# Gate and up products of 20 of 22 feature blocks per feed-forward as seven half-size block products instead of eight

## The chip, the cores and the metric

The kernel runs on one core of one Trainium2 chip. The metric is the device time of one execution in microseconds (us). The kernel before takes 1288.24 us, the median of 3 runs that lie between 1288.08 and 1288.88.

A core has engines that run side by side, each with its own queue, which it works through strictly in order: PE multiplies matrices (PEld is its weight load, which overlaps its products), DVE (VectorE), ACT (ScalarE) and POOL (GpSimd) work on elements, SP issues most DMAs. An instruction whose input is not ready holds up everything behind it on its engine.

## The reference, cut to what matters

The reference is an encoder of two layers in float32, for 512 tokens of 1024 features. Each layer is attention and then a feed-forward with 2816 hidden features:

```
def rmsnorm(x, g):
    y = xf * lax.rsqrt(jnp.mean(xf * xf, axis=-1, keepdims=True) + NORM_EPS)
    return y * g

def swiglu(hn, w_in, w_out):
    gate, up = jnp.split(hn @ w_in, 2, axis=-1)
    return (jax.nn.silu(gate) * up) @ w_out

for layer in range(DEPTH):            # 2
    x = x + attention of rmsnorm(x)   # latent + dilated windows in layer 0, grouped queries in layer 1
    x = x + swiglu(rmsnorm(x, ffn_norm[layer]), ffn_w_in[layer], ffn_w_out[layer])
return rmsnorm(x, final_norm)
```

`hn @ w_in` is 512 x 1024 times 1024 x 5632, twice: this is the product that the change computes in another way.

## The kernel before, in words

Features lie on the 128 partitions, the 512 tokens in the free dimension, so a token array is 8 tiles of 128x512. Every product is made from operands in two parts, high and low (`split`, `load`, `mm3` in lines 144 to 167): high x high, high x low, low x high, each a matmul that accumulates into one PSUM bank. Weights come in blocks of 128x1024 by one DMA into `wraw` (2 buffers); ACT makes the high part `whi` (line 154), POOL the low part `wlo` (line 155); `whi` and `wlo` have 3 buffers each.

The feed-forward (`ffn`) goes over 22 blocks of 128 hidden features in three groups of 8, 7 and 7 (`FGROUPS`). For a block f it makes the gate and the up product (`proj`, 24 matmuls of 512 columns each: 8 blocks of input features x 3), multiplies both by `rb` (one over the root mean square of every token, spread over all partitions), applies Silu, and splits the result. After a group come 8 output products with `ffn_w_out`. The gain of the norm is in the inputs already, the root mean square is not: so products start from `x` times gain while the sum of squares is still being added up on POOL, and `rb` comes later. The steps to `rb` are: the squares added (line 196, POOL), summed over partitions (line 213, PE), scaled (line 216, DVE), raised to -1/2 (line 218, POOL), spread (line 225, PE), copied (line 228, ACT).

The last group of layer 1 goes to `tokens_out`, which makes the last output product with tokens on partitions and the final norm.

The order of instructions on each engine is written by a scheduler when the kernel is built, from the program's order, priorities and its own estimates of durations; tiles of one tag share a place, and a new tile of a tag waits until the old one has been read for the last time.

Of the kernel before, what the change touches and what calls it, by code (L numbers as in the profile page):

```python
# [93 lines left out]
def encoder_kernel(ctx: ExitStack, tc: tile.TileContext, a, out):  # L94
# [554 lines left out]
    def ffn(xt, nr, layer, hsets, tail=None):  # L649
        w1, w2 = a["ffn_w_in"][layer], a["ffn_w_out"][layer]  # L650
        xs = nr.parts
        rb = None
        for gi, (f0, f1) in enumerate(FGROUPS):
            hs = []
            for f in range(f0, f1):
                tags = (("s", "s"), ("pt", "acc"))[f] if f < 2 else ("acc", "acc")
                og = proj(load([wview(w1, 0, KB, f * P, (f + 1) * P)], KB), xs, tags[0])
                ou = proj(load([wview(w1, 0, KB, FF + f * P, FF + (f + 1) * P)], KB), xs, tags[1])
                if rb is None:
                    rb = nr.spread(nr.columns(DM))  # L660
# [274 lines left out]
```

## Time and profile before

| | |
|---|---|
| median of 3 runs | 1288.24 us |
| profiled execution, first to last instruction (span) | 1286.2 us |
| what lies around the span, median less span | 2.0 us |
| PE busy | 1265.6 us, 98% of the span |
| DVE busy | 593.6 us, 46% |
| ACT busy | 524.2 us, 41% |
| POOL busy | 656.6 us, 51% |

The times come from three runs without the profiler, the profile from one execution of its own; it has no time beside its span. A row of a timeline gives the start, the duration, the engine, the line, the operation with the tile that it writes and the tiles that it reads, and in brackets how long the engine had been idle and who released it. The matmul rows overlap, since the engine is pipelined: the pace of PE is the distance between two starts, not the duration of one.

### The profile page before, as it was taken

The numbers are of one execution on the slowest core, as the hardware profiler recorded it, in microseconds if no ns is written. First come the engines' busy times: TensorE is split into PE (matmuls) and PEld (weight loads), VectorE is DVE, ScalarE is ACT, GpSimd is POOL, SyncE is SP. The second block draws the span as 40 slices with busy tenths as digits, with TensorE's granted clock in tenths as the row PEclk, the third lists the DMA queues.
The fourth block names the chain that finished last, engine by engine and source line by source line (L and its number), as shares of the span: only waits on it lengthen the run. The fifth ranks groups of instructions, "written<-read, shape, count | busy, mean of one in ns | idle before, by whom it ended". The sixth has DMA issues, their size and how long they took to land.

```text
span 1286.2 us, 15919 instructions
## 1 busy us (share of the span) xinstructions
PE 1265.6 (98%) x5925; PEld 1023.1 (80%) x5925; DVE 593.6 (46%) x1037; ACT 524.2 (41%) x892; POOL 656.6 (51%) x406
## 2 busy tenths in 40 slices
PE   8999999999999999999999999999999999999997
PEld 7877788787788888888889877787788888888886
DVE  4543347975333133213354878997333123313333
ACT  5324346864332123222243577675432123222242
POOL 5644334545644444444466787766644444444450
PEclk9999999999999999999999999999999999999999
DMA  9333333113332333232332520203233233233331
GB/s 281 83 100 108 77 70 109 48 50 92 99 98 82 106 90 96 86 109 87 91 101 86 139 63 23 71 24 94 83 99 97 85 97 99 88 92 98 98 99 66
DMA packets 200717, 117.88 MB, mean 92 GB/s; under 512 B 15890, under 2 KB 192064, under 8 KB 200640
## 3 DMA queue, kind: packets, MB, share of 16 engines
q1 hardware_dynamic: 198864, 113.69, 30.8%
q10 hardware_dynamic: 1776, 3.17, 0.7%
q8 instruction: 47, 0.77, 0.3%
q14 instruction: 30, 0.25, 0.1%
HBM read 106.09 MB, written 4.19 MB: 86 GB/s over the span
## 4 chain that ended last, share of the span: by engine, by line
PE 91%; DVE 3%; POOL 2%; DMA 2%; ACT 1%; issue 1%; SPq 0%; POOLq 0%; ACTq 0%; DVEq 0%
PE ps_acc L165 24%; PE ps_acc L166 24%; PE ps_acc L167 24%; PE ps_pt L338 3%; PE ps_o L366 2%; PE ps_s L166 2%; PE ps_s L167 2%; PE ps_s L165 2%; PE ps_o L365 2%; POOL wlo L155 1%; PE ps_s L825 1%; PE ps_s L826 1%; PE ps_s L490 1%; PE ps_o L522 1%; DMA m<-e 1%
## 5 line engine op out<-in xcount | busy, mean ns | idle before, releaser
L155 POOL TENSOR_TENSOR wlo<-wraw,whi 128x1024 fp32r<-128x1024 f32 (+3 forms) x194 | 444.7, 2295 | 441.3 <-ACT whi L154 438.0
L154 ACT CAST whi<-wraw 128x1024 fp32r<-128x1024 f32 (+3 forms) x194 | 188.4, 971 | 529.3 <-PE ps_acc L166 461.9
L165 PE MATMUL ps_acc<-x,whi 128*128 128x512 f32 x672 | 266.6, 397 | 2.0 <-DVE x L357 1.6
L167 PE MATMUL ps_acc<-x,wlo 128*128 128x512 f32 x672 | 266.5, 397 | 0.0
L166 PE MATMUL ps_acc<-x,whi 128*128 128x512 f32 x672 | 266.4, 397 | 0.0
L165 PE MATMUL ps_acc<-b,whi 128*128 128x512 f32 x448 | 177.1, 395 | 0.0
L166 PE MATMUL ps_acc<-b,whi 128*128 128x512 f32 x448 | 176.6, 395 | 0.0
L167 PE MATMUL ps_acc<-b,wlo 128*128 128x512 f32 x448 | 176.6, 395 | 0.0
L165 PEld LDWEIGHTS ps_acc<-x,whi 128*128 128x128 f32 x672 | 126.4, 188 | 32.3 <-issue 1.4
L166 PEld LDWEIGHTS ps_acc<-x,whi 128*128 128x128 f32 x672 | 126.5, 188 | 29.0 <-DVE x L359 0.4
L167 PEld LDWEIGHTS ps_acc<-x,wlo 128*128 128x128 f32 x672 | 126.5, 188 | 29.0
L664 DVE TENSOR_TENSOR m<-ps_acc,rbc 128x512 f32<-128x512 f32 x42 | 29.0, 691 | 195.9 <-PE ps_acc L167 195.9
L165 PEld LDWEIGHTS ps_acc<-b,whi 128*128 128x128 f32 x448 | 84.0, 187 | 20.6
L167 PEld LDWEIGHTS ps_acc<-b,wlo 128*128 128x128 f32 x448 | 84.0, 187 | 20.6
L166 PEld LDWEIGHTS ps_acc<-b,whi 128*128 128x128 f32 x448 | 84.0, 187 | 20.4
L674 DVE TENSOR_TENSOR d<-d,ps_acc 128x512 f32<-128x512 f32 x40 | 27.5, 688 | 143.0 <-PE ps_acc L167 143.0
L179 DVE TENSOR_TENSOR b<-ps_pt,b 128x512 fp32r<-128x512 f32 x112 | 75.1, 682 | 17.2 <-ACT b L178 16.7
L178 ACT CAST b<-ps_pt 128x512 fp32r<-128x512 f32 x112 | 63.2, 584 | 25.1 <-PE ps_pt L338 24.3
L165 PE MATMUL ps_acc<-d,whi 128*128 128x512 f32 x160 | 63.2, 397 | 0.1
L167 PE MATMUL ps_acc<-d,wlo 128*128 128x512 f32 x160 | 62.5, 393 | 0.0
L196 POOL TENSOR_TENSOR nacc<-nacc,e 128x512 f32<-128x512 f32 x31 | 47.0, 1518 | 26.5 <-ACT e L195 26.0
L662 DVE TENSOR_TENSOR m<-ps_acc,rbc 128x512 f32<-128x512 f32 x40 | 27.7, 691 | 65.2 <-PE ps_acc L167 65.2
(326 smaller groups left out, 2041.2 us busy)
## 6 DMA issues: line engine op xcount, KB each, us to landing
wraw<-in_ffn_w_in_dram SPq DMA_DIRECT2D x88, 512.0 KB, 3.8
wraw<-in_ffn_w_out_dram SPq DMA_DIRECT2D x23, 512.0 KB, 3.5
wraw<-in_w_in_ab_dram SPq DMA_DIRECT2D x21, 512.0 KB, 3.9
wraw<-in_ffn_w_out_dram SPq DMA_DIRECT2D x24, 448.0 KB, 3.4
wraw<-in_gqa_w_q_dram SPq DMA_DIRECT2D x8, 512.0 KB, 3.6
wraw<-in_gqa_w_o_dram SPq DMA_DIRECT2D x16, 192.0 KB, 2.4
bias<-in_c_bias_dram SPq DMA_DIRECT2D x4, 576.0 KB, 4.2
b<-in_x_dram SPq DMA_DIRECT2D x4, 512.0 KB, 6.5
```

The lines of the kernel that those rows point to most:

```text
L154: nc.scalar.copy(h, r)
L155: nc.gpsimd.tensor_sub(l, r, h.bitcast(F32))
L165: nc.tensor.matmul(dst, lhsT=lhs[0], rhs=rhs[0], start=first, stop=False)
L166: nc.tensor.matmul(dst, lhsT=lhs[0], rhs=rhs[1], start=False, stop=False)
L167: nc.tensor.matmul(dst, lhsT=lhs[1], rhs=rhs[0], start=False, stop=last)
L178: nc.scalar.copy(hi, src)
L179: nc.vector.tensor_sub(lo, src, hi.bitcast(F32))
L196: nc.gpsimd.tensor_add(self.acc, self.acc, sq)
L338: nc.tensor.transpose(pt[:, k * P:(k + 1) * P], p[:, k * P:(k + 1) * P], ident)
L662: nc.vector.tensor_mul(gg, og, rb)
L664: nc.vector.tensor_mul(uu, ou, rb)
L674: nc.vector.tensor_add(xt[n], xt[n], o)
```

## The change

Per feed-forward, blocks f = 0 and 1 are computed as before (but with the sign turned); the other 20 by `seven`. It takes gate and up weights of a block as a 2 x 2 matrix (gate or up, input features 0 to 511 or 512 to 1023) and the inputs as another (input features, tokens 0 to 255 or 256 to 511), and uses Strassen's scheme in Winograd's form: seven products of half size, each 4 x 3 matmuls of 256 columns, in place of eight. Sums of weights (`sab`, `sdc`) and of inputs (`combine`) are needed for it. The sums are made in float32 and split afterwards. `combine` needs `rb` before it can start, since the inputs have to be normalised now; it runs once per feed-forward, after block 0. The groups become (0 to 8, 8 to 16, 16 to 22) in layer 0 and (0 to 8, 8 to 14, 14 to 18, 18 to 22) in layer 1, and up to four output products of the last group stand behind a block of the next one.

```
+    def combine(xt, rb, gk):
...
+        cb = {n: [] for n in ("b11", "b21", "b22", "t1", "t2", "t3", "t4")}
+        H = T // 2
+        for i in range(4):
+            g1, g2 = gain(gk, i), gain(gk, i + 4)
+            ya, yb = U(f"m{4 + 2 * (i % 2)}"), U(f"m{5 + 2 * (i % 2)}")
+            nc.vector.tensor_mul(ya, xt[i], rb)
+            nc.vector.tensor_mul(yb, xt[i + 4], rb)
+            y11 = E()[:, 0:H]
+            tt = U(("tab", "bias")[i % 2], shape=((P, 2, T), (P, 9 * P))[i % 2])
...
+            nc.scalar.activation(y11, ya[:, 0:H], AF.Copy, scale=g1)
+            nc.vector.scalar_tensor_tensor(tt[:, 0:H], ya[:, H:T], g1, y11, op0=ALU.mult, op1=ALU.subtract)
+            nc.vector.scalar_tensor_tensor(tt[:, H:T], yb[:, H:T], g2, tt[:, 0:H], op0=ALU.mult, op1=ALU.subtract)
+            nc.vector.tensor_sub(tt[:, T:T + H], y11, tt[:, H:T])
+            nc.vector.scalar_tensor_tensor(tt[:, T + H:2 * T], yb[:, 0:H], g2, tt[:, H:T],
+                                           op0=ALU.mult, op1=ALU.subtract)
...
+            split(bh, bl, y11)
+            cb["b11"].append((bh, bl))
+            h, l = U(f"d{2 * i}", F32R), U(f"d{2 * i + 1}", F32R)
+            nc.scalar.activation(h, yb, AF.Copy, scale=g2)
+            nc.vector.scalar_tensor_tensor(l, yb, g2, h.bitcast(F32), op0=ALU.mult, op1=ALU.subtract)
+            cb["b21"].append((h[:, 0:H], l[:, 0:H]))
+            cb["b22"].append((h[:, H:T], l[:, H:T]))
+            for j in range(2):
+                h, l = U(f"x{4 * i + 2 * j}", F32R), U(f"x{4 * i + 2 * j + 1}", F32R)
+                src = tt[:, j * T:(j + 1) * T]
+                nc.scalar.activation(h, src, AF.Copy, scale=-1.0)
+                nc.vector.scalar_tensor_tensor(l, src, -1.0, h.bitcast(F32), op0=ALU.mult, op1=ALU.subtract)
...
+    def seven(w1, f, cb):
...
+        def parts(src, hi, lo):
+            nc.scalar.copy(hi, src)
+            nc.vector.tensor_sub(lo, src, hi.bitcast(F32))
+            return hi, lo
...
+        rg = U("wraw", bufs=2, shape=(P, WCOLS))
+        nc.sync.dma_start(rg.rearrange("p (k n) -> p k n", k=KB), wview(w1, 0, KB, f * P, (f + 1) * P))
+        u1, u2 = U(f"m{4 + 2 * (f % 2)}"), U(f"m{5 + 2 * (f % 2)}")
+        for h, u in enumerate((u1, u2)):
+            nc.sync.dma_start(u.rearrange("p (k n) -> p k n", k=4),
+                              wview(w1, 4 * h, 4 * h + 4, FF + f * P, FF + (f + 1) * P))
...
+        gh, gl = parts(rg, U("whi", F32R, bufs=3, shape=(P, WCOLS)), U("wlo", F32R, bufs=3, shape=(P, WCOLS)))
+        nc.vector.tensor_add(sab[:, 0], u1, u2)
+        nc.vector.tensor_add(sab[:, 1], sab[:, 0], g1)
+        ah, al = parts(sab.rearrange("p a b -> p (a b)"), U("whi", F32R, bufs=3, shape=(P, WCOLS)),
+                       U("wlo", F32R, bufs=3, shape=(P, WCOLS)))
+        nc.vector.tensor_add(sdc[:, 0], sab[:, 1], g2)
+        nc.vector.tensor_add(sdc[:, 1], u1, g1)
+        dh, dl = parts(sdc.rearrange("p a b -> p (a b)"), U("whi", F32R, bufs=3, shape=(P, WCOLS)),
+                       U("wlo", F32R, bufs=3, shape=(P, WCOLS)))
+        uh, ul = U("oT", F32R, bufs=2), U(("m12", "otmp")[f % 2], F32R)
+        nc.scalar.copy(uh, u2)
+        nc.gpsimd.tensor_sub(ul, u2, uh.bitcast(F32))
...
+        def product(o, h, l, half, name, first):
+            for i in range(4):
+                c = slice(half * T + i * P, half * T + (i + 1) * P)
+                x = cb[name][i]
+                for j, (wt, xp) in enumerate(((h, x[0]), (h, x[1]), (l, x[0]))):
+                    nc.tensor.matmul(o[:, 0:H], lhsT=wt[:, c], rhs=xp, start=first and i == 0 and j == 0,
+                                     stop=i == 3 and j == 2, skip_group_check=True)
...
+        product(r1, gh, gl, 0, "b11", True)
+        nc.scalar.copy(e[:, 0:H], r1[:, 0:H])
+        yield None
+        r2 = psum("acc")
+        product(r2, gh, gl, 1, "b21", True)
+        nc.vector.tensor_add(gg[:, 0:H], r2[:, 0:H], e[:, 0:H])
+        r3 = psum("pt")
+        product(r3, ah, al, 0, "t1", True)
+        nc.scalar.copy(e[:, T:T + H], r3[:, 0:H])
+        product(r1, ah, al, 1, "t2", False)
+        nc.scalar.copy(e[:, H:T], r1[:, 0:H])
+        product(r3, dh, dl, 0, "b22", False)
+        nc.vector.tensor_add(gg[:, H:T], r3[:, 0:H], e[:, H:T])
+        nc.scalar.activation(gg, gg, AF.Silu)
+        product(r1, dh, dl, 1, "t3", False)
+        nc.vector.tensor_add(uu[:, H:T], r1[:, 0:H], e[:, T:T + H])
+        yield None
+        product(r1, uh, ul, 0, "t4", False)
+        nc.vector.tensor_mul(uu[:, 0:H], r1[:, 0:H], gg[:, 0:H])
+        nc.vector.tensor_mul(uu[:, H:T], uu[:, H:T], gg[:, H:T])
+        yield uu
...
+        def finish(f, unit):
+            uu = next(unit)
+            hs[f] = slot(f)
+            split(*hs[f], uu)
...
+        todo, open_ = [], None
+        for gi, (f0, f1) in enumerate(groups):
+            for f in range(max(f0, FIRST), f1):
+                unit = seven(w1, f, cb)
+                next(unit)
+                if open_ is not None:
+                    finish(*open_)
+                next(unit)
+                open_ = f, unit
+                if f > f0:
+                    for _ in range(min(len(todo), 4)):
+                        out_block(*todo.pop(0))
...
     def tokens_out(hs, f0):
...
-                    nc.gpsimd.tensor_sub(t[2 + h], r, t[h].bitcast(F32))
...
+            nc.vector.tensor_sub(t[:, 2:4], r, t[:, 0:2].bitcast(F32))
```

`product` makes 12 matmuls of 256 columns (line 725 of the changed kernel). The inputs of the classic blocks now lie in the large tiles `b0` to `b3` in both layers. Block 2 stands for the first block by `seven` below.

Where it stands on the engines, first PE in layer 0, between the four classic products and what follows them; the rows give line, operation, written tile, read tiles, size, and the engines waited for. Before:

```order
L167 MATMUL ps_acc_3179<-x7_2758,wlo_3175 128x512
L225 MATMUL ps_o_3125<-ident_72,rcol_3123 128x128 [waits Pool_49]
L225 MATMUL ps_o_3125<-ident_72,rcol_3123 128x128 x3
L165 MATMUL ps_acc_3218<-x0_2744,whi_3213 128x512 [waits Activation_49]
L166 MATMUL ps_acc_3218<-x8_2745,whi_3213 128x512
L167 MATMUL ps_acc_3218<-x0_2744,wlo_3214 128x512
```

and now:

```order
L167 MATMUL ps_acc_3271<-b1_2937,wlo_3267 128x512
L225 MATMUL ps_o_3113<-ident_72,rcol_3111 128x128 [waits Pool_49]
L225 MATMUL ps_o_3113<-ident_72,rcol_3111 128x128 x3
L725 MATMUL ps_s_3334<-d16_3141,whi_3314 128x256 [waits DVE_49,Activation_49]
L725 MATMUL ps_acc_3351<-d0_3145,whi_3314 128x256 [waits Activation_49]
L725 MATMUL ps_s_3334<-d17_3142,whi_3314 128x256 [waits DVE_49]
```

Before, PE went straight on to block 2 after line 225, with inputs `x` that it had; now what follows line 225 reads `d16`, `d17`, `d0` and so on, which `combine` writes.

DVE at the same place. Before, `rb` (`rbc`) is used by the multiplications of blocks 0 and 1, and then DVE waits for PE:

```order
L202 SCALAR_TENSOR_TENSOR x15_2759<-d15_2735,gcol_65,x7_2758 128x512 [waits Activation_49]
L216 TENSOR_SCALAR tiny_3121<-ps_o_3116 128x4 [waits PE_49]
L662 TENSOR_TENSOR m8_3132<-ps_s_3060,rbc_3130 128x512 [waits Activation_49]
L664 TENSOR_TENSOR m10_3133<-ps_s_3091,rbc_3130 128x512
L662 TENSOR_TENSOR m9_3204<-ps_pt_3148,rbc_3130 128x512 [waits PE_49]
```

Now a low part of 128x1024 stands ahead of line 216, which is on the way to `rb`:

```order
L695 TENSOR_TENSOR wlo_3315<-wraw_3306,whi_3314 128x1024 [waits PE_49,DMAHW6_49,Activation_49,Pool_49]
L216 TENSOR_SCALAR tiny_3109<-ps_o_3104 128x4 [waits PE_49]
L763 TENSOR_TENSOR m8_3120<-ps_s_3048,rbc_3118 128x512 [waits Activation_49]
L765 TENSOR_TENSOR m10_3121<-ps_s_3079,rbc_3118 128x512
L659 TENSOR_TENSOR m4_3130<-d8_2728,rbc_3118 128x512 [waits DMAHW3_49]
L660 TENSOR_TENSOR m5_3131<-d12_2732,rbc_3118 128x512 [waits DMAHW7_49,DMAHW5_49,DMAHW3_49]
```

and from `m8_3120<-ps_s_3048,rbc_3118`, the first that needs `rb`, to the low part `wlo_3321` DVE has 54 instructions, which end so:

```order
L684 SCALAR_TENSOR_TENSOR x9_3202<-tab_3187,x8_3201 128x512 [waits DMAHW4_49,Activation_49]
L684 SCALAR_TENSOR_TENSOR x13_3227<-bias_3214,x12_3226 128x512 [waits DMAHW0_49,Activation_49]
L684 SCALAR_TENSOR_TENSOR x11_3206<-tab_3187,x10_3205 128x512 [waits Activation_49]
L684 SCALAR_TENSOR_TENSOR x15_3231<-bias_3214,x14_3230 128x512 [waits Activation_49]
L708 TENSOR_TENSOR tab_3312<-m4_3308,m5_3309 128x512 [waits DMAHW2_49,DMAHW0_49,DVE_49]
L713 TENSOR_TENSOR bias_3313<-m4_3308,wraw_3306 128x512 [waits DVE_49]
L709 TENSOR_TENSOR tab_3312<-tab_3312,wraw_3306 128x512 [waits DVE_49]
L712 TENSOR_TENSOR bias_3313<-tab_3312,wraw_3306 128x512 [waits DVE_49]
L695 TENSOR_TENSOR wlo_3321<-tab_3312,whi_3320 128x1024 [waits Activation_49,Pool_49]
```

The sums of block 2's weights use the tiles `tab` and `bias`, in which `combine` keeps its sums, and so stand behind all of `combine`. PE waits for the last of these rows here, after 28 matmuls of block 2 (24 with the gate weights, 4 with the high part of the sums):

```order
L725 MATMUL ps_pt_3365<-x0_3149,whi_3320 128x256 [waits Activation_49]
L725 MATMUL ps_pt_3365<-x1_3150,whi_3320 128x256
L725 MATMUL ps_s_3334<-x0_3149,whi_3320 128x256
L725 MATMUL ps_s_3334<-x1_3150,whi_3320 128x256
L725 MATMUL ps_pt_3365<-x0_3149,wlo_3321 128x256 [waits DVE_49]
L725 MATMUL ps_pt_3365<-x4_3174,whi_3320 128x256
```

All that is left of block 2 and everything behind it on PE stands behind that wait. In layer 1 the order is the same, except that line 225 has 9 classic matmuls behind it.

Last, what DVE does for one block further on (block 7 is being prepared, block 6 is on PE, block 5 is finished). Before, a block had four instructions on DVE (lines 662, 664, 665 and 179); now it has 13, of which the last, a split of 128x512 (line 179), is not shown:

```order
L708 TENSOR_TENSOR tab_3943<-m6_3939,m7_3940 128x512 [waits DMAHW7_49,DMAHW5_49,DVE_49]
L709 TENSOR_TENSOR tab_3943<-tab_3943,wraw_3937 128x512 [waits DMAHW6_49,DVE_49]
L745 TENSOR_TENSOR m11_3709<-ps_s_3706,p_3707 128x256 [waits PE_49]
L749 TENSOR_TENSOR m11_3709<-m11_3709,m9_3708 128x256 [waits DVE_49,Activation_49]
L695 TENSOR_TENSOR wlo_3829<-bias_3815,whi_3828 128x1024 [waits Activation_49]
L695 TENSOR_TENSOR wlo_3946<-wraw_3937,whi_3945 128x1024 [waits PE_49,Activation_49]
L735 TENSOR_TENSOR m8_3838<-ps_acc_3869,p_3837 128x256 [waits Activation_49]
L712 TENSOR_TENSOR bias_3944<-tab_3943,wraw_3937 128x512 [waits DVE_49]
L713 TENSOR_TENSOR bias_3944<-m6_3939,wraw_3937 128x512
L748 TENSOR_TENSOR m11_3709<-ps_s_3706,m9_3708 128x256 [waits PE_49]
L695 TENSOR_TENSOR wlo_3952<-tab_3943,whi_3951 128x1024 [waits PE_49,Activation_49]
L742 TENSOR_TENSOR m8_3838<-ps_pt_3883,p_3837 128x256 [waits PE_49,Activation_49]
```

The low parts of the input weights have moved from POOL to DVE; POOL keeps one of 128x512 per block (line 718) and those of the output weights (line 155).

## Rows read from the trace of the kernel before

**Rows 1.** The page: span and instructions, busy time, the chain's lines.

```profile
span 1286.2 us, 15919 instructions
...
PE 1265.6 (98%) x5925; PEld 1023.1 (80%) x5925; DVE 593.6 (46%) x1037; ACT 524.2 (41%) x892; POOL 656.6 (51%) x406
...
PE ps_acc L165 24%; PE ps_acc L166 24%; PE ps_acc L167 24%; PE ps_pt L338 3%; PE ps_o L366 2%; PE ps_s L166 2%; PE ps_s L167 2%; PE ps_s L165 2%; PE ps_o L365 2%; POOL wlo L155 1%; PE ps_s L825 1%; PE ps_s L826 1%; PE ps_s L490 1%; PE ps_o L522 1%; DMA m<-e 1%
```

**Rows 2.** Timeline, DVE and POOL, feed-forward of layer 0: start us, us, what.

```profile
500.53 0.69 DVE L662 TENSOR_TENSOR m<-ps_acc,rbc 128x512 f32<-128x512 f32 x1 [1.30 <-PE ps_acc L167]
...
508.31 2.12 DVE L179 TENSOR_TENSOR m<-m,d 128x512 fp32r<-128x512 f32 x1 [0.69 <-ACT d L178]
511.73 0.69 DVE L662 TENSOR_TENSOR m<-ps_acc,rbc 128x512 f32<-128x512 f32 x1 [1.30 <-PE ps_acc L167]
...
507.07 2.82 POOL L155 TENSOR_TENSOR wlo<-wraw,whi 128x1024 fp32r<-128x1024 f32 x1 [3.20 <-ACT whi L154]
```

**Rows 3.** Timeline, PE, keys of layer 1: first and last of 28 matmuls.

```profile
684.78 0.28 PE L167 MATMUL ps_s<-whi,x 128*128 128x256 f32 x1
...
687.98 0.28 PE L167 MATMUL ps_s<-whi,x 128*128 128x256 f32 x1
```

**Rows 4.** Timeline, PE, DVE and POOL around `rb` in layer 0.

```profile
337.32 1.05 PE L225 MATMUL ps_o<-ident,rcol 128*128 128x128 f32 x8
338.13 0.47 PE L165 MATMUL ps_acc<-x,whi 128*128 128x512 f32 x1
...
331.61 0.16 DVE L216 TENSOR_SCALAR tiny<-ps_o 128x4 f32<-128x4 f32 x1 [6.97 <-PE ps_o L213]
339.03 0.69 DVE L662 TENSOR_TENSOR m<-ps_s,rbc 128x512 f32<-128x512 f32 x1 [7.26 <-ACT rbc L228]
339.63 0.68 DVE L664 TENSOR_TENSOR m<-ps_s,rbc 128x512 f32<-128x512 f32 x1
...
329.04 2.39 POOL L155 TENSOR_TENSOR wlo<-wraw,whi 128x1024 fp32r<-128x1024 f32 x1 [0.29 <-ACT whi L154]
331.84 1.02 POOL L218 TENSOR_TENSOR rcol<-tiny,mhalf 128x4 f32<-128x4 f32 x1 [0.41 <-DVE tiny L216]
```

**Rows 5.** The page, DMA issues: KB each, us to landing.

```profile
wraw<-in_ffn_w_in_dram SPq DMA_DIRECT2D x88, 512.0 KB, 3.8
...
d<-xsp SPq DMA_DIRECT2D x8, 256.0 KB, 3.4
```

**Rows 6.** Groups by form and single rows: what one operation takes.

```profile
L154 ACT CAST whi<-wraw 128x1024 fp32r<-128x1024 f32 x140 | 147.0, 1051 | 423.0 <-PE ps_acc L166 373.6 <-DMA wraw<-in_ffn_w_in_dram 16.1 <-PE ps_pt L166 13.7
L179 DVE TENSOR_TENSOR x<-ps_acc,x 128x256 fp32r<-128x256 f32 x8 | 3.3, 418 | 1.0 <-ACT x L178 1.0
...
714.52 1.21 DVE L752 TENSOR_TENSOR b<-b,m 128x1024 f32<-128x1024 f32 x1
317.67 0.75 DVE L202 SCALAR_TENSOR_TENSOR x<-d,gcol,x 128x512 fp32r<-128x512 f32 x1 [0.79 <-ACT x L201]
312.08 1.29 POOL L196 TENSOR_TENSOR nacc<-nacc,e 128x512 f32<-128x512 f32 x1 [0.88 <-ACT e L195]
```

**Rows 7.** Timeline, POOL, PE and DVE around `rb` in layer 1.

```profile
915.13 2.39 POOL L155 TENSOR_TENSOR wlo<-wraw,whi 128x1024 fp32r<-128x1024 f32 x1 [1.10 <-ACT whi L154]
...
925.80 1.05 PE L225 MATMUL ps_o<-ident,rcol 128*128 128x128 f32 x8
...
927.51 0.69 DVE L662 TENSOR_TENSOR m<-ps_s,rbc 128x512 f32<-128x512 f32 x1 [7.28 <-ACT rbc L228]
```

**Rows 8.** PE after its first wait, then windows: us, five engines' busy (x), PEclk, DMA, GB/s.

```profile
9.44 1.08 PE L269 MATMUL ps_o<-ident,b 128*128 128x128 f32 x4 [2.93 <-DMA b<-in_x_dram]
...
10.00:12.00 2.00, 2.00 (x9) 1.83 (x8) 1.24 (x3) 1.44 (x3) 0.00 (x0) 0.50 1.11 342
12.00:14.00 2.00, 2.00 (x9) 1.63 (x8) 2.00 (x5) 1.84 (x4) 0.08 (x1) 0.84 1.19 304
684.78:690.71 5.93, 5.93 (x52) 5.93 (x51) 2.66 (x2) 1.61 (x3) 4.08 (x2) 1.00 0.49 157
```

More of the change, by code (lines that the diff above doesn't have):

```diff
@@ L647, in mix_last @@
             nr.feed(xt[n], gain(g, n))
-    def ffn(xt, nr, layer, hsets, tail=None):
-        w1, w2 = a["ffn_w_in"][layer], a["ffn_w_out"][layer]
[L651 to L660, printed above, removed]
-                gg, uu = U(f"m{8 + f % 2}"), U(f"m{10 + f % 2}")
-                nc.vector.tensor_mul(gg, og, rb)
-                nc.scalar.activation(gg, gg, AF.Silu)
-                nc.vector.tensor_mul(uu, ou, rb)
-                nc.vector.tensor_mul(uu, uu, gg)
-                h, l = hsets[gi % 2](f - f0)
-                split(h, l, uu)
-                hs.append((h, l))
-            if tail is not None and gi == len(FGROUPS) - 1:
-                tail(hs, f0)
-                return
-            for n in range(KB):
-                o = proj(load([wview(w2, f0, f1, n * P, (n + 1) * P)], f1 - f0), hs)
-                nc.vector.tensor_add(xt[n], xt[n], o)
-                if gi == len(FGROUPS) - 1:
-                    yield n
@@ new lines, in ffn, with out_block @@
+    def ffn(xt, nr, layer, groups, slot, tail=None):
+        w1, w2 = a["ffn_w_in"][layer], a["ffn_w_out"][layer]
+        xs, hs = nr.parts, {}
+        for f in range(FIRST):
+            tags = (("s", "s"), ("pt", "acc"))[f]
+            og = proj(load([wview(w1, 0, KB, f * P, (f + 1) * P)], KB), xs, tags[0])
+            ou = proj(load([wview(w1, 0, KB, FF + f * P, FF + (f + 1) * P)], KB), xs, tags[1])
+            if f == 0:
+                rb = nr.spread(nr.columns(DM))
+            gg, uu = U(f"m{8 + f % 2}"), U(f"m{10 + f % 2}")
+            nc.vector.tensor_mul(gg, og, rb)
+            nc.scalar.activation(gg, gg, AF.Silu)
+            nc.vector.tensor_mul(uu, ou, rb)
+            nc.vector.scalar_tensor_tensor(uu, uu, -1.0, gg, op0=ALU.mult, op1=ALU.mult)
+            hs[f] = slot(f)
+            split(*hs[f], uu)
+            if f == 0:
+                cb = combine(xt, rb, ("ffn_norm", layer))
+        def finish(f, unit):
+            uu = next(unit)
+            hs[f] = slot(f)
+            split(*hs[f], uu)
+        def out_block(f0, f1, n):
+            o = proj(load([wview(w2, f0, f1, n * P, (n + 1) * P)], f1 - f0), [hs[f] for f in range(f0, f1)])
+            nc.vector.tensor_sub(xt[n], xt[n], o)
+        todo, open_ = [], None
[10 more added lines that the diff above has]
+                        out_block(*todo.pop(0))
+            if gi == len(groups) - 1:
+                while todo:
+                    out_block(*todo.pop(0))
+                finish(*open_)
+                if tail is not None:
+                    tail([hs[f] for f in range(f0, f1)], f0)
+                    return
+                for n in range(KB):
+                    out_block(f0, f1, n)
+                    yield n
+            todo += [(f0, f1, n) for n in range(KB)]
@@ L681, in encoder_kernel, with slots, slot @@
+    def slots(after):
+        at = {}
+        def slot(f):
+            if f % 10 < 2 or f >= after:
+                m = 2 * (f % 2)
+                if f >= after + 2:
+                    return U("e", F32R, bufs=4), U("e", F32R, bufs=4)
+                return U(f"m{m}", F32R), U(f"m{m + 1}", F32R)
+            if f % 2 == 0:
+                at[0] = B((f - 2 - f // 10 * 2) // 2 % 4)
+            return at[0][:, 2 * (f % 2), :], at[0][:, 2 * (f % 2) + 1, :]
+        return slot
     xt = [U(f"d{8 + n}") for n in range(KB)]
@@ L846, in encoder_kernel @@
     steps.flush()
-    bx = [B(i) for i in range(4)]
-    nr = Norm([(bx[k // 4][:, k % 4, :], bx[2 + k // 4][:, k % 4, :]) for k in range(8)])
+    nr = split_inputs()
     mix_last(xt, a["gqa_w_o"][0], hd1, (6, 7), nr, ("ffn_norm", 1))
-    def x_set(i):
-        return U(f"x{i}", F32R), U(f"x{8 + i}", F32R)
     def tokens_out(hs, f0):
@@ L908, in tokens_out @@
             nc.sync.dma_start(ov[c][:, T:], ys[1])
-    for _ in ffn(xt, nr, 1, (x_set, dm_set), tokens_out):
+    for _ in ffn(xt, nr, 1, ((0, 8), (8, 14), (14, 18), (18, 22)), slots(18), tokens_out):
         pass
```

50 lines of the change are left out of this document (26 added, 24 removed).

## Prediction

> **What bounds the kernel now.** I read the page first: its engine line and its chain [rows 1]. PE is busy for 98% of a span of 1286.2 us, and three lines, the three matmuls of `mm3`, hold 72% of the chain that ended last. No other engine is busy for more than 51%. So time goes away where PE gets less to do, and comes where PE waits. Next I read the feed-forward's timeline. Two calls of line 662 on DVE, one per feature block, start at 500.53 and 511.73 [rows 2]: a block of gate and up, 48 matmuls of 512 columns, takes 11.20 us, or 0.2333 us per matmul with all that stands between, and DVE waits for PE in it. Then I looked for matmuls of 256 columns with a new weight load each: the keys of layer 1 have them. 28 start between 684.78 and 687.98 [rows 3], which is 27 steps of 0.1185 us, at a granted clock of 1.00 [rows 8]. Last I read the way to `rb` in both layers [rows 4, 7], because `combine` hangs on it.
>
> **The products.** Seven products of 12 matmuls are 84 matmuls of 256 columns: 84 x 0.1185 = 9.95 us against 11.20. That takes 1.25 us off each of 40 blocks (20 in each of two layers): 50.0 us less. An eighth of the work would be 1.40 us; the rest is lost because two short matmuls take 0.237 us and one long 0.233.
>
> One rule speaks against short matmuls. The Trainium skill (TensorE: Matmul & The Clock Gate, section LDWEIGHTS) gives a weight load of 128 columns 107 ns, whatever follows it, and 256 columns at full clock about as much: if the two did not overlap, a block would take some 18 us by an estimate from that page. The trace of the keys, one load per matmul, does not agree with such a sum: 0.1185 us holds both.
>
> **The wait for the input sums.** Before, PE started block 2 at 338.13, right behind line 225 (337.32), since products need no `rb` [rows 4]. Now everything behind line 225 reads what `combine` writes. PE can do 28 matmuls of block 2 as the parts come (28 x 0.1185 = 3.3 us) and then waits for DVE's low part `wlo_3321`, the last of 54 DVE instructions that begin when `rb` is there. Nothing else is queued on PE that could go ahead; no output product exists yet, since group 0 is not finished. So this wait is bare.
>
> How long are the 54? They are 18 two-tensor operations of 512 columns at 0.69 (line 662, [rows 2]); 14 of scalar_tensor_tensor with 512 at 0.75 [rows 6]; 9 two-tensor of 256 at 0.42 [rows 6]; 12 scalar_tensor_tensor of 256, at 0.48 (0.75 less the 0.27 by which 0.69 and 0.42 differ); one of 1024 at 1.21 [rows 6]. The sum is 12.4 + 10.5 + 3.8 + 5.8 + 1.2 = 33.7 us. From it goes an overlap: where one does not need the other, the next starts after 0.60 instead of 0.69 (339.03 to 339.63, [rows 4]); for some 40 of the 54 that is 3.6. To it come waits: the high part of the weight sums on ACT (1.05, [rows 6]) stands between the last two steps with only 0.69 of DVE work beside it, 0.6 with the signals; two round trips to ACT for the first parts of `combine`, some 0.8; and two subtractions on POOL (line 718, 1.29 each by line 196's row, [rows 6]), which become ready in just this stretch and hold DVE up: line 179 took 2.12 instead of 0.69 while POOL was at work from 507.07 to 509.89 [rows 2]. That is 2.6. Together 34.1; I take 34. Both ends: 28.8, if all overlap and nothing waits, and 37.7, if nothing overlaps. The four loads of half weights into the tiles that `combine` used (256 KB, 3.4 us, [rows 5]) start when its sums are done with them and have some 3.7 us of DVE work beside them: I count them at nothing; without that cover they cost up to 1.
>
> Layer 0 has one more step. Line 216, on the way to `rb`, now stands behind block 2's first low part on DVE. That one needs its DMA, whose place POOL frees at 329.04 + 2.39 = 331.4; 3.8 later [rows 5] the weights are there, 1.05 for ACT, 1.21 for DVE: 337.5. Line 216 then starts at 337.6 instead of 331.61; POOL's power ends 1.25 after that start (331.61 to 332.86, [rows 4]), at 338.9; line 225 starts at 339.0 with the signal, and `rb` comes 1.71 behind the start of line 225 (337.32 to 339.03): 340.7 instead of 339.03. In layer 1 the same steps give 915.13 + 2.39 + 3.8 + 1.05 + 1.21 + 1.4 = 925.0, earlier than line 225's 925.80 [rows 7]: no delay, `rb` at 927.51.
>
> So PE's loss is, in layer 0, 340.7 + 34 - 338.1 - 3.3 = 33.3; in layer 1, 927.5 + 34 - 926.6 - 3.3 = 31.6 (926.6 is line 225 plus the 0.81 that it took in layer 0). Together 64.9 us, with ends of 52.8 (28.8 each, no delay of `rb`) and 72.3.
>
> **The clock after it.** After PE's first wait in the kernel, for the inputs, the granted clock is 0.50 from 10 to 12 us and 0.84 from 12 to 14 [rows 8]: half speed from 9.44 to some 12.6, 3.2 us, in which half is lost. Each of the two long waits should leave the same behind: 2 x 1.6, I take 3.0, between 0 and 4.
>
> **The blocks in steady state.** DVE's 13 instructions per block are 3 of 1024, 5 of 512 and 5 of 256 columns: 3.6 + 3.5 + 2.1 = 9.2 us, 8.0 if all overlap; plus up to 1.29 for POOL's subtraction: between 9.3 and 10.5, beside PE's 9.95. Weights have places for one block ahead, and each low part has 4 us or more between the end of the product that frees its place and its own use, with 1.05 on ACT and 1.21 on DVE to do. So PE sets the pace, but narrowly: I take 0.1 us of wait per block, 4 us for 40, between 0 and 22 (0.55 each). The output products between blocks (24 matmuls, 5.6 us of PE each, with one subtraction on DVE) give DVE time to catch up. ACT has some 6 us per block (three of 1.05 and smaller ones), which is not the bound.
>
> **The end.** The last group has 4 blocks instead of 7; the low parts of its output weights are now DVE's (4 x 1.21), in line with the last block's own work, while before POOL had most of them. I take 1 us, between 0 and 4. The groups change nothing in the number of output products' matmuls, and signs cost nothing, being in operations that exist.
>
> **The sum.** -50.0 + 64.9 + 3.0 + 4 + 1 = +22.9 us against the profiled execution's span of 1286.2: 1309.1. The median of the runs stands 2.0 above that span, so I predict 1311 us. The likeliest case's own range is 1299 to 1322.
>
> **Rivals.** First, DVE becomes the bound in steady state. For it: 10.5 us of instructions and POOL waits against 9.95, nearly every one with a wait on another engine. Against it: DVE overlaps operations whose wait is over, as at 339.63. If every POOL subtraction is paid in full and nothing overlaps, a block takes 10.5, and 22 stands in place of 4: 1329. The Trainium skill (SBUF — State Buffer, section Who interferes with whom) has the rule behind this: a DVE operation with two SBUF inputs and a POOL operation that reads SBUF shut each other out for their whole length. By that rule each block pays up to 1.29; the 2.12 us row agrees.
>
> Second, the other side: the wait is shorter than what the products save. It decides at 24 us for the 54 instructions: then PE's loss in a layer is about 22 to 23 and falls under the 25.0 that 20 blocks save. DVE would have to run at the slope between 256 and 512 columns alone (0.27 per 256): 54 instructions would then take 23.6, the losses would be 22.9 and 21.2, and with the clock staying up and no waits the time 1282, faster. For it: DVE's fixed part is hidden in part where rows overlap. Against it: the rows overlap by 0.09, not by 0.15 or more, and some steps need one another. Halfway, at 26 to 28 us and with no other cost, it is no change.
>
> Third, that PE fills the wait with something else. The order of the changed kernel excludes it: PE is strictly in order, and block 2's matmuls stand at the head. That the seven products aren't what PE does is excluded there too: 84 matmuls per block stand in PE's queue.
>
> **How the numbers follow.** Forecast 0.68; DVE as the bound 0.21; a short wait 0.11, of which 0.06 ends faster and 0.05 at no change. Within 0.2%, 2.6 us, a measurement of this kernel can't tell a change. That gives faster 0.06, same 0.05, slower 0.89. The range goes from 1292, where all of the first wait's low ends meet (52.8 - 50.0 = +2.8) and nothing else is lost, to 1333, where DVE bounds the blocks and the wait is at its middle or a little above; both waits at 37.7 with slow blocks would be beyond it.
>
> **What would show it.** Products: line 725's starts 0.1185 apart, and a block every 9.95 us or a little more where no output product stands between. The wait: two gaps of some 30 us on PE, only 28 short matmuls in each, from about 339 and 928, ended by line 695 on DVE; DVE without a pause there. Line 216 in layer 0 behind line 695, near 337.7. The granted clock at half for some 3 us after each gap. Steady state: PE's idle time before line 725 small, with DVE line 745 or 695 as releaser; if it is half a microsecond a block, the first rival holds. The prediction is wrong if these gaps are under 25 us, or if blocks take more than 10.5.

## The result, and the profile after

The changed kernel takes 1302.88 us, the median of 4 runs between 1302.14 and 1303.70; the kernel before took 1288.16 in 4 runs on the same chip. The ratio is 1.0116, with a 95% interval from 1.0102 to 1.0130: slower by 14.7 us, where 22.8 were forecast. The profiled execution has a span of 1301.6 against 1286.2.

The page of the changed kernel, engine line, clock row and chain:

```profile
span 1301.6 us, 19664 instructions
...
PE 1238.0 (95%) x7365; PEld 1073.8 (83%) x7365; DVE 850.3 (65%) x1488; ACT 646.3 (50%) x1133; POOL 507.0 (39%) x364
...
PEclk9999999999779999999999999999959999999999
...
PE 86%; DVE 8%; ACT 2%; POOL 1%; DMA 1%; issue 1%; SPq 0%; POOLq 0%; DVEq 0%; ACTq 0%
```

PE is busy for 27.6 us less than before [rows 1] and yet the kernel is longer. The clock row has two dents, one in each layer, and DVE now holds 8% of the chain, against 3% before. What PE waits for, by releaser (us in total, times, longest):

```profile
PE ps_pt L725 <- ACT whi L694: 14.2, 2, 7.1
PE ps_s L725 <- DVE d L179: 11.5, 6, 3.0
PE ps_s L725 <- ACT d L178: 8.6, 4, 3.6
PE ps_acc L725 <- DVE d L677: 3.8, 4, 1.5
...
PE ps_pt L725 <- DVE wlo L695: 3.2, 2, 1.6
```

All five come in even numbers: the same wait, once per layer, in pieces. Layer 0 on PE's timeline (start, duration, what, idle time before and its releaser), the place of [rows 4]:

```profile
337.76 1.05 PE L225 MATMUL ps_o<-ident,rcol 128*128 128x128 f32 x8
342.45 0.58 PE L725 MATMUL ps_s<-d,whi 128*128 128x256 f32 x1 [3.63 <-ACT d L178]
...
359.84 0.41 PE L725 MATMUL ps_acc<-d,wlo 128*128 128x256 f32 x1
367.34 0.80 PE L725 MATMUL ps_pt<-x,whi 128*128 128x256 f32 x2 [7.08 <-ACT whi L694]
...
370.17 0.58 PE L725 MATMUL ps_pt<-x,wlo 128*128 128x256 f32 x1 [1.60 <-DVE wlo L695]
...
373.96 0.63 PE L725 MATMUL ps_s<-x,whi 128*128 128x256 f32 x2
374.39 0.41 PE L725 MATMUL ps_s<-x,wlo 128*128 128x256 f32 x1
...
375.33 0.40 PE L725 MATMUL ps_s<-d,whi 128*128 128x256 f32 x2
375.57 0.28 PE L725 MATMUL ps_s<-d,wlo 128*128 128x256 f32 x1
```

PE is free at 337.76 + 0.81 = 338.57 and gets its last missing part at 370.17. In between it does the 28 matmuls of the forecast, 3.3 us of work; so 28.3 us are lost. Behind the wait two matmuls take 0.43 us (373.96 to 374.39), from 374.9 on 0.24 (375.33 to 375.57): half clock for 4.7 us (granted 0.50, the lower of the two levels, 1.2 GHz), in which 22 matmuls are done that would take 2.6; 2.1 lost.

The same stretch on DVE and POOL, ahead of `rb` and at the end of `combine`:

```profile
329.79 1.23 DVE L695 TENSOR_TENSOR wlo<-wraw,whi 128x1024 fp32r<-128x1024 f32 x1 [4.74 <-ACT whi L694]
332.02 0.16 DVE L216 TENSOR_SCALAR tiny<-ps_o 128x4 f32<-128x4 f32 x1 [1.01 <-PE ps_o L213]
339.47 0.69 DVE L763 TENSOR_TENSOR m<-ps_s,rbc 128x512 f32<-128x512 f32 x1 [7.29 <-ACT rbc L228]
340.08 0.68 DVE L765 TENSOR_TENSOR m<-ps_s,rbc 128x512 f32<-128x512 f32 x1
...
357.88 0.47 DVE L665 SCALAR_TENSOR_TENSOR tab<-m,gcol,e 128x256 f32<-128x256 f32 x1
358.28 0.47 DVE L665 SCALAR_TENSOR_TENSOR bias<-m,gcol,e 128x256 f32<-128x256 f32 x1
...
366.24 1.65 DVE L712 TENSOR_TENSOR bias<-tab,wraw 128x512 f32<-128x512 f32 x1
367.82 2.30 DVE L695 TENSOR_TENSOR wlo<-tab,whi 128x1024 fp32r<-128x1024 f32 x1
364.69 2.65 POOL L718 TENSOR_TENSOR m<-m,oT 128x512 fp32r<-128x512 f32 x1 [31.41 <-ACT oT L717]
367.31 1.73 POOL L718 TENSOR_TENSOR otmp<-m,oT 128x512 fp32r<-128x512 f32 x1
```

No row between 339.47 and 370.12 has idle time in brackets: the 54 instructions fill 30.65 us without a gap. So DVE's amount of work sets the wait. POOL's two subtractions are in it: they lie over the last two rows, which take 1.65 and 2.30 where the same instructions take 0.69 (e8, below) and 1.23 (329.79) without POOL.

Windows (length; busy us and instructions of PE, PEld, DVE, ACT, POOL; granted clock; DMA share, GB/s) of the wait and of three blocks later on, then starts of line 748, one per block:

```profile
339.00:369.00 30.00, 9.68 (x28) 6.74 (x28) 29.49 (x54) 18.49 (x32) 4.31 (x2) 0.53 0.13 39
...
400.00:430.00 30.00, 30.00 (x255) 30.00 (x254) 28.49 (x39) 17.21 (x27) 5.23 (x3) 1.00 0.37 104
```

```profile
416.32 0.41 DVE L748 TENSOR_TENSOR m<-ps_s,m 128x256 f32<-128x256 f32 x1
426.31 0.41 DVE L748 TENSOR_TENSOR m<-ps_s,m 128x256 f32<-128x256 f32 x1
...
1014.89 0.41 DVE L748 TENSOR_TENSOR m<-ps_s,m 128x256 f32<-128x256 f32 x1
1024.95 0.41 DVE L748 TENSOR_TENSOR m<-ps_s,m 128x256 f32<-128x256 f32 x1
```

A block takes 9.99 us in layer 0 and 10.06 in layer 1, against 11.20 before [rows 2], and PE does not wait in it, although DVE is busy for 95%.

Four more places on PE: the start of layer 1's keys, `rb` of layer 1, the end of the wait there, and the end of layer 0's last block:

```profile
694.51 0.28 PE L167 MATMUL ps_s<-whi,x 128*128 128x256 f32 x1
...
936.96 1.05 PE L225 MATMUL ps_o<-ident,rcol 128*128 128x128 f32 x8
...
939.72 0.39 PE L167 MATMUL ps_acc<-b,wlo 128*128 128x512 f32 x1
...
969.37 0.58 PE L725 MATMUL ps_pt<-x,wlo 128*128 128x256 f32 x1 [1.61 <-DVE wlo L695]
...
665.00 0.28 PE L725 MATMUL ps_s<-x,otmp 128*128 128x256 f32 x1
666.44 0.73 PE L165 MATMUL ps_acc<-m,whi 128*128 128x512 f32 x2 [1.17 <-ACT m L178]
```

With the same points of before (337.32, 684.78 and 925.80 in [rows 4, 3, 7]) the difference of the spans splits so: up to line 225 of layer 0 +0.44; from there to the keys 356.75 - 347.46 = +9.29; to line 225 of layer 1 242.45 - 241.02 = +1.43; from there to the end 364.64 - 360.40 = +4.24. Together +15.4.

### The profile page after: what moved, and what is told of

The parts are those of the page before. It is cut to its first block, busy times and chain, and to the rows that moved or that the text cites. A ratio compares the mean times of both kernels' runs of the same rounds, so it can differ in the third digit from the quotient of the medians.

```text
span 1301.6 us, 19664 instructions
## 1 busy us (share of the span) xinstructions
PE 1238.0 (95%) x7365; PEld 1073.8 (83%) x7365; DVE 850.3 (65%) x1488; ACT 646.3 (50%) x1133; POOL 507.0 (39%) x364
## 4 chain that ended last, share of the span: by engine, by line
PE 86%; DVE 8%; ACT 2%; POOL 1%; DMA 1%; issue 1%; SPq 0%; POOLq 0%; DVEq 0%; ACTq 0%
PE ps_s L725 17%; PE ps_acc L165 12%; PE ps_acc L166 12%; PE ps_acc L167 12%; PE ps_pt L725 9%; PE ps_acc L725 4%; PE ps_pt L338 3%; PE ps_o L366 2%; PE ps_o L365 1%; PE ps_s L166 1%; PE ps_s L165 1%; PE ps_s L167 1%; DVE b L202 1%; PE ps_s L961 1%; PE ps_s L490 1%
## 5 line engine op out<-in xcount | busy, mean ns | idle before, releaser
L155 POOL TENSOR_TENSOR wlo<-wraw,whi 128x1024 fp32r<-128x1024 f32 (+4 forms) x122 | 246.9, 2029 | 197.3 <-ACT whi L154 181.1
L154 ACT CAST whi<-wraw 128x1024 fp32r<-128x1024 f32 (+4 forms) x122 | 107.8, 889 | 152.0 <-PE ps_acc L166 60.4
L725 PE MATMUL ps_s<-x,whi 128*128 128x256 f32 x640 | 119.7, 284 | 0.0
L165 PE MATMUL ps_acc<-x,whi 128*128 128x512 f32 x280 | 111.8, 401 | 2.2 <-DVE x L357 1.6
L167 PE MATMUL ps_acc<-x,wlo 128*128 128x512 f32 x280 | 112.0, 400 | 0.0
L166 PE MATMUL ps_acc<-x,whi 128*128 128x512 f32 x280 | 111.9, 400 | 0.0
L725 PEld LDWEIGHTS ps_s<-x,whi 128*128 128x128 f32 x640 | 101.0, 191 | 1.6
L165 PE MATMUL ps_acc<-b,whi 128*128 128x512 f32 x256 | 101.4, 396 | 0.3 <-DVE d L779 0.3
L167 PE MATMUL ps_acc<-b,wlo 128*128 128x512 f32 x256 | 101.2, 395 | 0.0
L166 PE MATMUL ps_acc<-b,whi 128*128 128x512 f32 x256 | 100.9, 394 | 0.0
L725 PE MATMUL ps_s<-x,wlo 128*128 128x256 f32 x320 | 90.8, 284 | 0.0
L725 PE MATMUL ps_s<-d,whi 128*128 128x256 f32 x320 | 68.0, 293 | 20.1 <-DVE d L179 11.5
```

The source lines that it names most:

```text
L154: nc.scalar.copy(h, r)
L155: nc.gpsimd.tensor_sub(l, r, h.bitcast(F32))
L165: nc.tensor.matmul(dst, lhsT=lhs[0], rhs=rhs[0], start=first, stop=False)
L166: nc.tensor.matmul(dst, lhsT=lhs[0], rhs=rhs[1], start=False, stop=False)
L167: nc.tensor.matmul(dst, lhsT=lhs[1], rhs=rhs[0], start=False, stop=last)
L725: nc.tensor.matmul(o[:, 0:H], lhsT=wt[:, c], rhs=xp, start=first and i == 0 and j == 0, stop=i == 3 and j == 2, skip_group_check=True)
```

## Experiments

Theory A: two bare waits of PE for DVE's input sums behind `rb`, with the half clock behind them, eat what the products save. Its rivals, as the expectations name them: B, a good part is lost in the blocks; C, round trips between the engines set the wait, not DVE's amount of work; D and E, on how DVE's chain grows when PE gets more to do meanwhile.

**e1, no input sums.** The input sums and their low parts are left out: `combine` became plain copies on ACT, 24 of 512 columns and 8 of 256:

```
-            nc.vector.tensor_mul(ya, xt[i], rb)
...
+            for t in (h, l):
+                nc.scalar.activation(t, xt[i + 4], AF.Copy, scale=g2)
```

> This kernel leaves the input sums out: the operands of the seven products are plain copies of the residual times gain that ACT makes, without rb, without sums and without low parts from DVE, so they are there before the first seven products are due; the number and the shapes of PE's matmuls are those of the changed kernel. Theory A (PE waits for DVE's chain behind rb, and for nothing else that matters): both waits of 28.3 and 26.1 us and the half clock behind them (2.1 and 1.1) go, 1302.9 - 57.6 = 1245 us, between 1240 and 1251. Theory B (a good part of what the seven products should save is also lost in the blocks themselves, to DVE, POOL and ACT work beside them, and would stay): 1258 or more.

Measured: 1264.2 us (ratio to before 0.9813, 0.9798 to 0.9828). By its numbers that speaks for B, but the run has a wait of its own, since the copies stood on ACT among the squares that `rb` needs and ahead of the high parts that block 1 of the classic blocks needs. ACT is full here while PE has half its time idle:

```profile
330.00:340.00 10.00, 4.65 (x19) 3.75 (x20) 0.16 (x1) 9.96 (x16) 3.78 (x3) 0.66 0.01 2
```

So it settled nothing, and e5 repeats it.

**e5, no input sums, again.** All products read one pair of copies made by DVE:

```
+        h, l = U("x0", F32R), U("x1", F32R)
+        for t in (h, l):
+            nc.vector.tensor_copy(t, xt[7])
```

> As the first of these kernels, but mended: there the 24 copies on ACT stood ahead of the high parts of block 1's weights, and PE waited for these some 11 us in each layer. Now all seven products read one pair of copies that DVE makes (2 instructions instead of the input sums); what the kernel computes for the 20 blocks is left meaningless, the number and the shapes of PE's matmuls are the same. Theory A (both waits and the clock behind them are all that stands against the saving): 1302.9 - 57.6 = 1245 us, up to 1251 if block 2's high and low parts, whose tiles block 1 frees only at its end, come up to 3 us late in each layer. Theory B (a loss that stays in the blocks): 1256 or more.

Measured: 1253.2 us (0.9729, 0.9712 to 0.9745), 2 above the upper end of theory A. PE's two rows before block 1, and the window in which PE waited for `combine` before:

```profile
327.91 0.79 PE L166 MATMUL ps_s<-b,whi 128*128 128x512 f32 x1 [2.87 <-DVE b L202]
...
897.49 0.80 PE L166 MATMUL ps_s<-b,whi 128*128 128x512 f32 x1 [3.96 <-DVE b L202]
...
338.00:369.00 31.00, 31.00 (x247) 30.22 (x246) 26.71 (x40) 18.00 (x28) 2.81 (x2) 1.00 0.29 81
```

The window is full, at full clock. The two copies delayed line 202 instead: 2.87 and 3.96 of wait where the changed kernel has 1.29 and 1.31, 4.2 us, and half clock for some 3 us behind each, some 3.0 lost, of which the changed kernel has 1.4 in layer 1 as well. Without what is new here it would be some 1247.4, inside A's range. B is out: seven products in 40 blocks lose nothing that would show beside the wait.

**e2, weight sums first.** Tiles `p` and `e` in `combine` instead of `tab` and `bias`, and block 2's weight sums ahead of it in the program:

```
+        ahead = seven(w1, FIRST, got)
+        next(ahead)
+        got.append(combine(xt, rb, ("ffn_norm", layer)))
```

> The first block's weight sums and low parts get tiles of their own and stand ahead of the input sums on DVE; the input sums use other tiles (p and e in place of tab and bias). Theory A: DVE's chain behind rb is bound by how much DVE has to do, so five instructions less in it (364.33 to 370.12 in layer 0, 5.8 us, of which about 2 come back because the two low parts wait for tiles that PE frees only at the end of block 1) make each wait some 3.8 shorter: 1302.9 - 7.6 = 1295, between 1290 and 1299. Theory C (the wait's length comes from round trips between DVE, ACT and PE rather than from DVE's amount of work): no change, 1301 to 1305.

Measured: 1288.1 us (0.9992, 0.9983 to 1.0001), equal to the kernel before, and 14.8 below the changed kernel, twice what was expected and just below A's range. C is out. Why A's number was too small is read from the trace: the order of the parts counts, not their sum alone (e9 tests this). The window of layer 0's wait in this run:

```profile
339.00:364.00 25.00, 13.76 (x45) 10.02 (x44) 24.60 (x48) 16.10 (x28) 0.00 (x0) 0.59 0.09 24
```

With both weight sums there, every input part that DVE finishes gives PE matmuls at once. Some 45 matmuls are begun by 364, where the changed kernel had done 28 by 370 and had the other 56 of the block still ahead.

**e3, four classic blocks** (`FIRST = 4`, else as in the changed kernel; the products of blocks 2 and 3 go to `e` tiles).

> Four classic blocks instead of two ahead of the first seven products, so PE has 22.4 us more to do while DVE makes the input sums; 18 blocks by seven products in each layer. Theory A: two more classic blocks cost 2 x 1.17 in each layer, 4.7 together; DVE's chain grows by their 8 instructions (4.8) and by what POOL's low parts of their weights hold it up (2 to 8), so that of the waits of 28.3 and 26.1 some 14 each are left; 1302.9 + 4.7 - 26.4 - 1 = 1280, between 1272 and 1292. Theory B (the loss is in the blocks): 1300 or more, since there are fewer blocks but the same losses. Theory D (cover counts in full, DVE's chain doesn't grow): 1302.9 + 4.7 - 44.8 = 1263.

Measured: 1281.8 us (0.9955, 0.9938 to 0.9972), as A says. B and D are out.

**e4, five classic blocks** with the order of e2:

```
-FIRST = 2
+FIRST = 5
```

> Five classic blocks, with the tiles of e2 and the weight sums ahead of the input sums in the program; 17 blocks by seven products in each layer. Theory A: three more classic blocks cost 3 x 1.17 in each layer, 7.0; the cover of 33.6 us is longer than the wait of 28, but DVE's chain grows by 12 instructions (7.2) and by POOL's low parts, so some 4 us of wait are left in each layer: 1302.9 + 7.0 - 46.4 - 2 = 1262, between 1253 and 1273, faster than the kernel before. Theory E (DVE's chain grows as fast as the cover, since POOL's low parts shut it out): 1280 or more.

Measured: 1264.1 us (0.9812, 0.9797 to 0.9827): it beats the kernel before by 24.5 us. PE is never idle until 374 and loses a few us after:

```profile
340.00:374.00 34.00, 34.00 (x150) 27.44 (x150) 33.00 (x51) 19.77 (x32) 10.14 (x4) 1.00 0.35 101
374.00:386.00 12.00, 9.57 (x53) 8.37 (x52) 12.00 (x19) 6.82 (x11) 2.12 (x1) 0.74 0.22 62
```

**e6, six classic blocks**, as e4.

> Six classic blocks ahead (16 by seven products in each layer), otherwise as with five. In the run with five, PE still lost 6.3 us in layer 0 and some 8 in layer 1 behind the classic blocks, waits and half clock together. Theory A: 11.2 us more of cover, of which DVE's chain takes back 2.4 for its instructions and 2 to 4 for POOL's low parts, end all of it; the sixth block costs 1.17 in each layer: 1264.1 - 14 + 2.3 = 1252, between 1249 and 1258. Theory E (DVE's chain grows as fast as the cover): 1264 to 1267.

Measured: 1269.8 us (0.9854, 0.9839 to 0.9869), 5.7 above e4. My expectation fell, and E's number is nearer, for another reason than E's. DVE in this run:

```profile
356.52 0.69 DVE L760 TENSOR_TENSOR m<-ps_pt,rbc 128x512 f32<-128x512 f32 x1 [4.11 <-PE ps_pt L167]
...
362.12 0.69 DVE L762 TENSOR_TENSOR m<-ps_acc,rbc 128x512 f32<-128x512 f32 x1 [4.91 <-PE ps_acc L167]
...
367.72 0.69 DVE L760 TENSOR_TENSOR m<-ps_acc,rbc 128x512 f32<-128x512 f32 x1 [4.10 <-PE ps_acc L167]
369.75 1.86 DVE L708 TENSOR_TENSOR tab<-tab,wraw 128x512 f32<-128x512 f32 x1 [1.33 <-DMA wraw<-in_ffn_w_in_dram]
```

DVE stands idle for 14.5 us in the middle of `combine`: the multiplications that take up later classic blocks' products, and a weight sum whose load is late, stand ahead of the remaining input sums in its queue. PE gave DVE the time, and DVE's order threw it away: behind the classic blocks PE loses some 14 us in the two layers, against 13 in e4. Of the 5.3 us by which the two spans differ (1268.7 and 1263.4) some 2.3 are the price of the sixth block in two layers and 1.5 a fall of the clock that comes and goes between executions (see "Not foreseen" below).

**e9, five blocks, sums in the old order** (`combine` again behind block 0, block 5's weight sums behind it; tiles in `combine` as in e2, and block 4's result in a `b` tile).

> Five classic blocks and the tiles of e2 for the input sums, but the input sums stand again behind block 0 in the program and the weight sums of the first block by seven products behind them, as in the changed kernel. What it tells apart: with six blocks DVE stood idle for 4.91, 4.10 and 1.33 us, since its queue had products of later classic blocks and weight sums whose load was still under way ahead of the remaining input sums. Theory A with the queue (DVE's order decides once the cover is long enough): here most input sums stand ahead of those, DVE's chain ends some 3 us earlier than in e4: 1264.1 - 4 = 1260, between 1255 and 1266. If only the amount of DVE's work counts: 1264, as in e4.

Measured: 1270.6 us (0.9862, 0.9846 to 0.9878), 6.5 above e4, of which some 1.5 are the same fall of the clock; this expectation fell too. With the weight sums last, PE has again a bare wait for them:

```profile
380.32 0.80 PE L724 MATMUL ps_pt<-x,whi 128*128 128x256 f32 x2 [5.77 <-ACT whi L693]
383.54 0.58 PE L724 MATMUL ps_pt<-x,wlo 128*128 128x256 f32 x1 [1.99 <-DVE wlo L694]
```

It is e2's lesson from the other side: with the same work on DVE, what PE can use first has to come first. No run has both, the weight sums first and the input sums ahead of the later classic blocks, so what DVE's idle time in e6 costs by itself is not shown.

**e7, e4 with the low parts of classic blocks 2 to 4 on DVE**, and **e10, the same in e9**:

```
-        nc.gpsimd.tensor_sub(l, r, h.bitcast(F32))
+        (nc.vector if quick else nc.gpsimd).tensor_sub(l, r, h.bitcast(F32))
```

> As with five classic blocks, but the low parts of the weights of classic blocks 2 to 4 are made by DVE (1.13 us each beside other DVE work) instead of POOL. Theory A with the lock (while POOL subtracts two SBUF tiles, a DVE instruction that reads two SBUF tiles stands still: 2.90, 2.62 and 2.33 us in the run with five blocks instead of 0.74, 0.48 and 0.68): three to five such stops of about 2 us go, as many instructions of 1.13 come, so the chain ends 2 to 4 us earlier in each layer: 1264.1 - 5 = 1259, between 1256 and 1262. Without a lock the chain grows by 4 to 6 us and the time with it: 1268 or more.

> As the run before with the low parts of classic blocks 2 to 4 on DVE. With the lock: stopped DVE instructions of 2 us go, DVE gets five instructions of 1.13; chain 1 to 3 us shorter in each layer, so 1256 to 1260 if e9 has 1260. If the chain waits for PE's last classic products anyway, no change against e9 within 2 us.

Measured: 1264.5 us (0.9810, 0.9781 to 0.9839) and 1269.4 us (0.9851, 0.9836 to 0.9865): neither differs from e4 and e9 by more than the intervals. The stopped rows are gone in e7 (line 676 takes 0.74), but five or so instructions of 1.13 stand in DVE's queue instead. The expected 5 us did not come; that it became clearly slower, as without a lock, did not come either. The four times of e7 lie between 1259.3 and 1267.4, so a gain or loss of 2 or 3 us is neither shown nor excluded. e10's 1.3 us is the "no change" of its expectation, but not for the reason given there: DVE hardly stands idle (0.99 us in the stretch).

**e8, line 718 on DVE**, else the changed kernel:

```
-        nc.gpsimd.tensor_sub(ul, u2, uh.bitcast(F32))
+        nc.vector.tensor_sub(ul, u2, uh.bitcast(F32))
```

> The changed kernel with POOL's one subtraction per block (line 718) on DVE. With the lock: the two stopped rows at the end of each wait (1.65 and 2.30 us) become 0.67 and 1.21, one or two instructions of 0.60 come, and in the blocks DVE gets 0.60 more but stands still 1.0 to 1.3 less, so PE keeps its pace: 1302.9 - 3 = 1300, between 1298 and 1303. Without a lock DVE's 9.5 us per block become 10.1 against PE's 9.98 and DVE sets the pace: 1304 to 1308.

Measured: 1302.15 us (1.0106, 1.0091 to 1.0121), inside the range with the lock, and no difference from the changed kernel. Line 712 at the end of the wait, and the window of the steady blocks:

```profile
368.96 0.69 DVE L712 TENSOR_TENSOR bias<-tab,wraw 128x512 f32<-128x512 f32 x1
...
400.00:430.00 30.00, 30.00 (x255) 30.00 (x254) 27.10 (x42) 16.91 (x27) 0.00 (x0) 1.00 0.37 104
```

DVE has three instructions more in 30 us and is busy for 1.39 less: POOL's subtraction had cost it more than the subtraction itself does. PE's count is the same 255, so DVE was not the bound. In the wait the two subtractions, now DVE's, and two short waits for ACT take back what the two stopped rows give: DVE's chain fills 30.65 us again (340.68 to 371.33).

## Why the forecast was right, and where its size was off

Slower was right, and for the reason given: two gaps on PE behind `rb`, 28 matmuls in each, ended by line 695. e5 shows that without them the change would be worth some 41 us, e4 how to get most of it. The terms of the sum, forecast and measured:

| term | forecast | measured |
|---|---|---|
| products | -50.0 | about -46 |
| the two waits | +64.9 | 28.3 + 26.1 = +54.4 |
| half clock behind them | +3.0 | 2.1 + 1.2 = +3.3 |
| steady blocks | +4 | 0 |
| the end | +1 | 0 |
| not foreseen | - | 2.1 at the end of layer 0, 1.4 ahead of `rb` in layer 1, 0.4 ahead of it in layer 0 |
| sum on the span | +22.9 | +15.4 |

The products' row is what the balance leaves: layer 0 has +9.29 = 28.3 + 2.1 + 2.1 less 23.2; layer 1 +4.24 = 26.1 + 1.2 less 23.1. Per block that is 1.16, between the 1.14 and 1.21 that the block periods give (11.20 less 10.06 and 9.99).

- **The wait** is the term that was off, by 10.5 us, in three places. The chain took 30.65 us instead of 34, 3.35 less in each layer. Some 1.5 of it are overlap: nearly every one of the 54 overlapped the next (340.08 - 339.47 = 0.61 for 512 columns, 358.28 - 357.88 = 0.40 for 256 of scalar_tensor_tensor), where I let 40 do so. Another 1.4 are the waits for ACT that I had added (0.6 and 0.8): no row stands idle. The rest is POOL's hold, 2.6 forecast and some 2.1 measured. The delay of `rb` in layer 0, 1.7, did not come: line 695 ran at 329.79 and line 216 at 332.02. I had taken the wrong place for block 2's weights: of the two places of `wraw`, the one that POOL had freed a low part earlier was used. And in layer 1 I forgot the nine classic matmuls behind line 225, up to 939.72, though the order shown ahead of the prediction has them: 2.1.
- **Products and steady blocks**: PE never waits in the window shown, with DVE at 95%, but a block takes 9.99 to 10.06 us instead of 9.95. So the products save less than forecast and the blocks lose nothing; that the two terms together come out at the forecast -46 is luck. The rival that DVE becomes the bound was wrong: its price, POOL's lock in full, was nearly right (by e8 the lock costs (1.39 + 3 x 0.60) / 3 = 1.06 us a block, against 1.29), but DVE's overlap made room for it. The Trainium skill (SBUF — State Buffer, section Who interferes with whom) has it that a DVE instruction with two SBUF inputs and a POOL instruction that reads SBUF contend; the stopped rows at the end of the wait (1.65 and 2.30) agree.
- **The end**: no loss shows. From the start of the last matmul the changed kernel needs 7.6 us (1294.04 to 1301.6), the one before 8.0 (1278.17 to 1286.2), and PE has no wait listed in the last 300 us of either.
- **Half clock**: right in sum. In layer 1 the two-matmul steps of 0.43 us end some 2.5 us behind 969.37, in which 11 matmuls are done that would take 1.3, so 1.2 is lost.
- **Not foreseen**: the last block of layer 0 has nothing of another group behind it, so PE waits for its split (1.17 at 666.44, and two smaller steps). In layer 1 the clock fell to 0.51 for some 3 us after a wait of 1.31 at 920.18, ahead of `rb`; the kernel before has a wait of the same length there (1.30 at 910.58) and no fall. Of the ten traces with this wait (all but e1 and e5) three have the fall, this one, e6 and e9; e8, the changed kernel but for one line, does not. So it need not be the change's, and some 1.5 us between two traces can be this alone. What decides it stays open.

Of the prediction's sums one is off without weight: its second rival's 23.6 us should be 24.0 (89 steps of 256 columns at 0.27).

What stays open besides is what of e4's remaining loss could go: PE still waits some 2 to 4 us in each layer behind the classic blocks, with half clock behind it.

## What to carry to other kernels

Before an algorithm that needs fewer products is put in, ask what must be ready before its first product that was not needed before, and on which engine that is made: here an eighth fewer columns in 40 blocks lost against a preparation of 30 us, made twice, for which the bound engine stood still. If the preparation cannot be shorter, keep enough of the old kind of work to lie beside it (five classic blocks instead of two, in e2's order, turn +1.2% into -1.9%), and order it so that the first finished piece already lets the bound engine work. More cover than that can cost: what the extra work queues on the preparing engine may stand in front of the preparation.
